# Strassen's scheme for the up projection of the last two token groups

## The chip, the cores and the metric

The kernel runs on one core of one Trainium2 chip. The metric is the device time of one execution in microseconds (us). All times below are of the whole program: one layer of a hybrid encoder on 2064 tokens (16 learned meta tokens and 2048 frames) of 1024 features.

## The reference

The layer has two halves. The first (two kinds of attention with one input and one output projection) is not touched by the change. The second is a gated network with a causal convolution of width 3 over the tokens:

```python
def _conv_ffn(x, w_in, conv_w, conv_b, w_out):
    h = x @ w_in                     # 1024 -> 5632: the up projection
    y = conv_b
    for i in range(CONV_W):          # three taps over tokens
        y = y + conv_w[i] * hp[:, i:i + L]   # hp: h after two zero tokens
    u, gt = jnp.split(y, 2, axis=-1)
    return (jax.nn.silu(gt) * u) @ w_out     # 2816 -> 1024: the down projection
```

It is applied to the normed stream after the attention's output projection `w_o` was added: `h = h + _conv_ffn(_rmsnorm(h, norm2_g[l]), ...)`. Everything is float32.

## The kernel before

TensorE multiplies in a reduced format (`float32r`), so each operand is split into two parts, `hi` (a cast on ScalarE) and `lo` (the rest, one subtraction on VectorE or GpSimd), and each product is made of three: hi·hi, hi·lo and lo·hi (`product`, L1091). A matmul has 128 rows of contraction, 128 output rows and up to 512 columns (tokens).

The tokens of the network's second half go in four groups (`FGROUPS`): 514, 512, 512 and 512 tokens. The first two run beside the second part of the attention; the last two run alone, from about 2,610 us to the end. A group does, in this order: the output projection `w_o` with the norm (8 blocks of 24 matmuls, then the normed activations as `xh` and `xl`), then 22 blocks f of the inner width in 11 pairs (`mlp`). `up(G, f)` makes two 128-row blocks of the up projection, u (block f) and g (block 22 + f): eight contraction tiles by three matmuls of 512 columns each, 48 in all for one f. Then come the convolution, the gate (tanh on ScalarE, two steps on VectorE) and the split of the result into `zh` and `zl`. `down(G, ...)` adds the pair's share to the 8 output blocks: 48 matmuls of 512 columns for a pair. The down of a pair is written behind the up of the next pair, and the last down of a group behind the `w_o` of the next group.

Weights come by SyncE's DMA queue as 128x1024 `ww_raw` tiles (512 KB; ring of 2) and are split whole into `ww_hi` and `ww_lo` (ring of 3). u and g need two of them for one f; the down needs two for a pair.

The state of the convolution between groups is in the tile `edge`: two columns for each block, already multiplied by the taps (four small GpSimd instructions for each block, L1179 to L1182).

The order of instructions on each engine is set by a list scheduler that plays the program, in its written order of priority, against a model of the engines; at run time each engine takes its instructions strictly in that order and waits at semaphores.

## Time and profile before

| | us |
|---|---|
| median of 3 runs | 3427.64 |
| lowest and highest run | 3419.93, 3429.69 |
| the profiled execution | 3421.68 |
| its span | 3419.8 |
| TensorE busy in the span | 3321.0 (97%) |
| VectorE, ScalarE, GpSimd busy | 2301.7, 1653.1, 1165.1 |
| granted TensorE clock, mean | 0.987 |

A span is the time from the first to the last instruction of the program. "PE" is TensorE, "PEld" its weight loads, "DVE" VectorE, "ACT" ScalarE, "POOL" GpSimd, "SP" SyncE. L1096 is a line of the kernel; every matmul of the second half has that one line, so they are told apart by their tiles: `pp<-xh,ww_hi` is an up projection of the last groups, `pr<-zh,ww_hi` a down projection. A matmul's recorded duration overlaps that of the next one; what a stream of them costs is read from start to start, or from the length of a run of them in the chain of waits.

### The profile page before, as it was taken

To read this page: it belongs to the slowest core of one execution; us is meant where nothing else is said; L and a number is where in the kernel's file an instruction comes from. 1 tells how busy PE (TensorE), PEld (TensorE's weight loads), DVE (VectorE), ACT (ScalarE), POOL (GpSimd) and SP (SyncE) were. 2 spreads that over 40 slices of the span, in tenths; PEclk is the share of its full clock that TensorE was granted. 3 is DMA by queue.
4 is the path that set the end of the run, shared out by engine and by line. 5 is a ranking of instruction groups with operands and counts; after the bars stand their busy time and mean duration, and the time that the engine had idled before them with its cause. 6 is when DMAs were issued, how large, how long until landed. Compare 5 with 4: busy or idle time off the path is not lost.

```text
span 3419.8 us, 62536 instructions
## 1 busy us (share of the span) xinstructions
PE 3321.0 (97%) x23259; PEld 2941.8 (86%) x23259; DVE 2301.7 (67%) x4849; ACT 1653.1 (48%) x3450; POOL 1165.1 (34%) x2055
## 2 busy tenths in 40 slices
PE   7999999999999999999999999999999999999999
PEld 7889888988988988999999998888887888878887
DVE  5655566566556657888878886777665666646666
ACT  5543444554244467765666665654333333333332
POOL 4441113344111167755444454422114211132121
PEclk9999999999999999999999999999999999999999
DMA  4556333355634255333333343223324323232222
GB/s 114 119 123 161 105 95 99 102 124 130 156 88 105 84 173 160 112 103 109 94 93 94 93 137 117 86 82 129 104 89 159 97 90 97 93 116 94 93 93 92
DMA packets 352888, 376.57 MB, mean 110 GB/s; under 512 B 169112, under 2 KB 281992, under 8 KB 351560
## 3 DMA queue, kind: packets, MB, share of 16 engines
q1 hardware_dynamic: 352392, 372.52, 38.2%
q8 instruction: 183, 3.00, 0.4%
q14 instruction: 121, 0.99, 0.1%
...
## 4 chain that ended last, share of the span: by engine, by line
PE 51%; DVE 2%; DMA 2%; POOL 2%; issue 2%; ACT 2%; SPq 0%; POOLq 0%; ACTq 0%; DVEq 0%
PE pp L1096 30%; PE pr L1096 12%; PE o L1022 3%; PE pt L1002 3%; DMA raw<-d_qk 2%; PE s L952 1%; PE s L954 1%; DVE ww_lo L82 1%; POOL xl L1158 0%; POOL kl L894 0%; DVE P L945 0%; DVE pl L1018 0%; ACT P L971 0%; DMA cb<-d_cd 0%; ACT ph L1017 0%
## 5 line engine op out<-in xcount | busy, mean ns | idle before, releaser
L82 DVE TENSOR_TENSOR ww_lo<-ww_raw,ww_hi 128x1024 fp32r<-128x1024 f32 (+1 forms) x304 | 375.4, 1244 | 248.7 <-PE pp L1096 128.9
L81 ACT CAST ww_hi<-ww_raw 128x1024 fp32r<-128x1024 f32 (+1 forms) x304 | 307.6, 1025 | 387.9 <-PE pp L1096 140.0
L1096 PE MATMUL pp<-xh,ww_hi 128*128 128x512 f32 (+2 forms) x1952 | 432.3, 353 | 11.4 <-ACT xh L1157 6.0
L1096 PE MATMUL pp<-xh,ww_lo 128*128 128x512 f32 (+2 forms) x1952 | 429.1, 351 | 0.0
L1096 PE MATMUL pp<-xl,ww_hi 128*128 128x512 f32 (+2 forms) x1952 | 428.4, 350 | 0.3 <-POOL xl L1158 0.3
L1096 PEld LDWEIGHTS pp<-xh,ww_hi 128*128 128x128 f32 x1952 | 324.8, 190 | 66.5 <-ACT xh L1157 11.1
L1096 PEld LDWEIGHTS pp<-xl,ww_hi 128*128 128x128 f32 x1952 | 326.2, 189 | 52.8 <-POOL xl L1158 1.0
L1096 PEld LDWEIGHTS pp<-xh,ww_lo 128*128 128x128 f32 x1952 | 325.3, 189 | 47.4
L1179 POOL TENSOR_SCALAR c<-c,pc 128x1 f32<-128x1 f32 x220 | 84.7, 385 | 611.2 <-ACT c L1176 609.8
L1018 DVE TENSOR_TENSOR pl<-pt,ph 128x512 fp32r<-128x512 f32 (+2 forms) x352 | 196.1, 562 | 51.7 <-ACT ph L1017 50.1
L1191 POOL TENSOR_TENSOR zl<-cv,zh 128x512 fp32r<-128x512 f32 (+1 forms) x110 | 119.8, 1089 | 312.7 <-ACT zh L1190 302.3
L945 DVE CUSTOM_DVE_ANT_0 P<-cb,s 16x16 f32<-16x16 f32 (+8 forms) x360 | 182.7, 519 | 53.6 <-PE s L954 29.1
L1017 ACT CAST ph<-pt 128x512 fp32r<-128x512 f32 (+2 forms) x352 | 167.8, 486 | 103.4 <-PE pt L1002 72.9
L1204 DVE TENSOR_TENSOR acc<-acc,pr 128x512 f32<-128x512 f32 x240 | 164.5, 688 | 73.5 <-PE pr L1096 69.1
L1002 PE MATMUL pt<-cst,P 128*128 128x128 f32 (+2 forms) x1224 | 202.6, 277 | 2.6 <-ACT P L971 1.5
L1173 ACT ACTIVATE cv<-pp,pc 128x510 f32<-128x510 f32 (+1 forms) x220 | 151.9, 691 | 84.3 <-PE pp L1096 82.9
L89 POOL TENSOR_TENSOR wi<-sq,kx 128x320 fp32r<-128x320 f32 (+2 forms) x48 | 48.2, 1003 | 389.9 <-ACT kx L88 290.1
L203 PE MATMUL pj<-xah,w_hi 128*128 128x384 f32 x480 | 165.8, 346 | 1.6 <-ACT xah L194 1.6
L1177 DVE SCALAR_TENSOR_TENSOR cv<-pp,pc,cv 128x511 f32<-128x511 f32 (+1 forms) x220 | 140.7, 639 | 36.0 <-ACT c L1176 35.9
L205 PE MATMUL pj<-xah,w_lo 128*128 128x384 f32 x480 | 164.4, 342 | 0.4 <-DVE w_lo L82 0.4
L204 PE MATMUL pj<-xal,w_hi 128*128 128x384 f32 x480 | 163.6, 341 | 0.0
L1022 PE MATMUL o<-ph,vs 128*128 128x256 f32 x576 | 158.1, 284 | 5.5 <-ACT ph L1017 5.2
...
## 6 DMA issues: line engine op xcount, KB each, us to landing
ww_raw<-in_fin_dram SPq DMA_DIRECT2D x176, 512.0 KB, 3.6
ww_raw<-in_fout_dram SPq DMA_DIRECT2D x88, 512.0 KB, 3.7
w_raw<-in_wt_dram SPq DMA_DIRECT2D x60, 512.0 KB, 3.8
...
ww_raw<-in_wo_dram SPq DMA_DIRECT2D x24, 512.0 KB, 3.6
...
```

The costliest lines, as they stand in the source:

```text
L81: nc.scalar.copy(hi, raw)
L82: nc.vector.tensor_sub(lo, raw, hi.bitcast(F32))
L203: nc.tensor.matmul(p, wh[:, c, :M], xh[:, c, :n], start=c == 0, stop=False)
L204: nc.tensor.matmul(p, wh[:, c, :M], xl[:, c, :n], start=False, stop=False)
L205: nc.tensor.matmul(p, wl[:, c, :M], xh[:, c, :n], start=False, stop=c == KC - 1)
L945: nc.vector.tensor_tensor_reduce(dst, c, src, 1.0, 3e38, op0=ALU.add, op1=ALU.min, accum_out=mx[:nq, np_ : np_ + 1])
L1002: nc.tensor.transpose(pt[:kn, x, c0 : c0 + nq], P[:nq, k0 : k0 + kn], K.ident[:nq, :nq])
L1017: nc.scalar.copy(ph[:kn, xs, c:N], pt[:kn, xs, c:N])
L1018: nc.vector.tensor_sub(pl[:kn, xs, c:N], pt[:kn, xs, c:N], ph[:kn, xs, c:N].bitcast(F32))
L1022: nc.tensor.matmul(o[:, c:N], vs[:kn, jj], pp[:kn, x, c:N], start=False, stop=jj == nt - 1 and y == 1)
L1096: self.K.nc.tensor.matmul(p, w, x, start=i == 0, stop=i == len(mms) - 1)
L1204: nc.vector.tensor_tensor(a, a, p, op=ALU.add)
```

## The change

For the last two groups (`win=True`) the up projection of one f is treated as a product of 2x2 blocks: the weights have rows u and g and two halves of the contraction (a11, a12 for u, a21, a22 for g), the activations two halves of the contraction and two halves of the tokens (b11 to b22). Strassen's scheme in Winograd's form gives the four result blocks from seven block products instead of eight, with sums of blocks before and after. A block product is 4 contraction tiles by three matmuls of 256 columns: 84 matmuls of 256 columns for one f, where there were 48 of 512.

- `operands`, once for a group: the four blocks of the normed activations are made in float32, four sums of blocks are formed on VectorE (t1 to t4), and the seven right-hand operands are split (`G.B`, seven hi and seven lo tiles of 128x1024; q0 to q6 are the hi parts, q7, q8, q12, q9, q14, q13, q10 the lo parts in the order of use).
- `up_win`, for each f: the two raw weight tiles `ru` (u) and `rg` (g) are loaded as before. Four sums of weight blocks are formed on GpSimd: s1 = a21 + a22 (L1252), then in place a21 = a11 - a21 (L1259), a11 = s1 - a11 (L1260), a12 = a12 - a11 (L1267). Seven 128x512 blocks w1 to w7 are split in four ring tiles (w1 and w5, w4 and w6, w2, w3 and w7); the lo parts of w6 and w3 are made on GpSimd, the others on VectorE. The seven products go to four PSUM banks of a ring of five. ScalarE (L1256, L1258, L1265, L1276) and VectorE (L1270, L1273, L1275, L1277) combine them into an SBUF tile `cc`, from which the convolution and the gate read.
- The edge is now the last two raw columns, copied in and out of `cc` by GpSimd (L1234, L1278); the second group writes it in that form (`carry`).
- `down` loads its weights in two halves of four output blocks, each from two DMAs of 256 KB, into a third raw buffer or the ring; the number of its matmuls is unchanged. The raw buffers are now three in turn; `ru` and `rg` are held until the sums and splits have read them.
- PSUM: `up` of these groups has the five banks and `down` the three, the other way round from before.

```diff
-        w = [self.weight(K.fout[f]) for f in fs]
+        w = [] if G.win else [self.weight(K.fout[f]) for f in fs]
...
+        nc.gpsimd.tensor_tensor(s1, a21, a22, op=ALU.add)
+        w1, w5 = pair((a11, nc.vector), (s1, nc.vector))
+        ba, bd = bank(), bank()
+        mm(ba, w1, B[0])
+        nc.scalar.copy(cu[:, lo], ba)
+        mm(bd, w5, B[1])
+        nc.scalar.copy(cg[:, hi], bd)
+        nc.gpsimd.tensor_sub(a21, a11, a21)
+        nc.gpsimd.tensor_sub(a11, s1, a11)
+        w4, w6 = pair((a22, nc.vector), (a11, nc.gpsimd))
+        bc = bank()
+        mm(bc, w4, B[2])
+        mm(ba, w6, B[3], False)
+        nc.scalar.copy(cu[:, hi], ba)
+        w2, = pair((a12, nc.vector))
+        nc.gpsimd.tensor_sub(a12, a12, a11)
+        bb = bank()
+        mm(bb, w2, B[4])
+        nc.vector.tensor_tensor(cu[:, lo], cu[:, lo], bb, op=ALU.add)
+        w3, w7 = pair((a12, nc.gpsimd), (a21, nc.vector))
+        mm(bd, w3, B[5], False)
+        nc.vector.tensor_tensor(cu[:, hi], cu[:, hi], bd, op=ALU.add)
+        mm(ba, w7, B[6], False)
+        nc.vector.tensor_tensor(cg[:, hi], cg[:, hi], ba, op=ALU.add)
+        nc.scalar.copy(cg[:, lo], ba)
+        nc.vector.tensor_tensor(cg[:, lo], cg[:, lo], bc, op=ALU.subtract)
+        nc.gpsimd.tensor_copy(edge, cc[:, :, 512:514])
...
+        for j, i in enumerate((f, FT + f)):
+            nc.scalar.activation(v[:, j], cc[:, j, 2:], AF.Identity, bias=pcol(K, "cb", i), scale=pcol(K, "cw2", i))
+            for k in (1, 0):
+                nc.vector.scalar_tensor_tensor(v[:, j], cc[:, j, k : k + 512], pcol(K, f"cw{k}", i), v[:, j], op0=ALU.mult, op1=ALU.add)
```

Two places show how the instructions stand. The first is GpSimd in the middle of the last group. Before, one f put this on it (`zl` of one f, then the four edge steps of a block of the next):

```order
L1191 TENSOR_TENSOR zl_6805_37482<-cv_6807_37508,zh_6804_37481 128x512
L1179 TENSOR_SCALAR c2_6837_37679<-c2_6837_37679,pc_11_70 128x1
L1180 TENSOR_SCALAR edge_2486_15450<-c2_6837_37679,pc_11_70 128x2
L1181 TENSOR_TENSOR edge_2486_15450<-edge_2486_15450,c2_6837_37679 128x1
L1182 TENSOR_TENSOR edge_2486_15450<-edge_2486_15450,pc_11_70 128x1
```

Now, from the last split of a pair's first f (the lo part of w3, `ww_lo_7140`) over its second f (raw tiles `ww_raw_7144` for u and `ww_raw_7145` for g; `sqv` is s1):

```order
L1245 TENSOR_TENSOR ww_lo_7140_40309<-ww_raw_7125_40213,ww_hi_7139_40308 128x512
L1252 TENSOR_TENSOR sqv_7146_40361<-ww_raw_7145_40358 128x512
L1278 COPY edge_2486_15450<-cc_7128_40218 128x2x2
L1259 TENSOR_TENSOR ww_raw_7145_40358<-ww_raw_7144_40357,ww_raw_7145_40358 128x512
L1260 TENSOR_TENSOR ww_raw_7144_40357<-sqv_7146_40361,ww_raw_7144_40357 128x512
L1267 TENSOR_TENSOR ww_raw_7144_40357<-ww_raw_7144_40357 128x512
L1245 TENSOR_TENSOR ww_lo_7153_40402<-ww_raw_7144_40357,ww_hi_7152_40401 128x512
L1234 COPY cc_7180_40584<-edge_2486_15450 128x2x2
L1245 TENSOR_TENSOR ww_lo_7159_40453<-ww_raw_7144_40357,ww_hi_7158_40452 128x512
L1290 TENSOR_TENSOR zl_7143_40354<-vv_7141_40343,zh_7142_40353 128x512
```

One 512-wide step for an f has become seven, and the copy of the first f's edge (L1278) stands between s1 and the other sums of the second f; it waits for VectorE's L1275 of the first f, the step that reads that f's last product. `ww_raw_7145` lies in the buffer that `ww_raw_7125` held, so its DMA waits for the first row.

The second place is TensorE at the same point. Before, one block of u and the block of g beside it:

```order
L1096 MATMUL pp_6835_37651<-xh_6512_35767,ww_hi_6828_37639 128x512 x8
L1096 MATMUL pp_6835_37651<-xl_6513_35768,ww_hi_6828_37639 128x512 x8
L1096 MATMUL pp_6835_37651<-xh_6512_35767,ww_lo_6829_37640 128x512 x8
L1096 MATMUL pp_6838_37687<-xh_6512_35767,ww_hi_6831_37645 128x512 x8
L1096 MATMUL pp_6838_37687<-xl_6513_35768,ww_hi_6831_37645 128x512 x8
L1096 MATMUL pp_6838_37687<-xh_6512_35767,ww_lo_6832_37646 128x512 x8
```

Now, from the lo part of the first f's w3 into the second f (`ww_hi_7148` holds w1 and w5 of the second f, `ww_hi_7152` w4 and w6, `ww_hi_7155` w2):

```order
L1109 MATMUL pr_7132_40228<-q5_6653_36903,ww_lo_7140_40309 128x256 x4
L1109 MATMUL pr_7131_40227<-q10_6656_36908,ww_hi_7139_40308 128x256 x2
L1109 MATMUL pr_7131_40227<-q6_6655_36907,ww_lo_7140_40309 128x256 x4
L1109 MATMUL pr_7150_40371<-q0_6640_36869,ww_lo_7149_40366 128x256 x4
L1109 MATMUL pr_7151_40372<-q1_6643_36883,ww_hi_7148_40365 128x256 x4
L1109 MATMUL pr_7151_40372<-q8_6644_36884,ww_hi_7148_40365 128x256 x4
L1109 MATMUL pr_7154_40407<-q2_6646_36889,ww_hi_7152_40401 128x256 x4
L1109 MATMUL pr_7154_40407<-q12_6647_36890,ww_hi_7152_40401 128x256 x4
L1109 MATMUL pr_7154_40407<-q2_6646_36889,ww_lo_7153_40402 128x256 x4
L1109 MATMUL pr_7157_40438<-q4_6651_36899,ww_hi_7155_40433 128x256 x4
L1109 MATMUL pr_7157_40438<-q14_6652_36900,ww_hi_7155_40433 128x256 x3
L1109 MATMUL pr_7151_40372<-q1_6643_36883,ww_lo_7149_40366 128x256 x4
```

The third row is the end of the first f's products. Behind the last row come the hi part of w6, its lo part (`ww_lo_7153`, made on GpSimd), the rest of w2 and w3; only then the first matmuls of a down projection. In the first f of a pair, 30 to 36 of the pair's 48 down matmuls stand between the up products.

## Rows read from the trace of the kernel before

**Rows 1.** The page: busy time of each engine; lines of the chain of waits.

```profile
PE 3321.0 (97%) x23259; PEld 2941.8 (86%) x23259; DVE 2301.7 (67%) x4849; ACT 1653.1 (48%) x3450; POOL 1165.1 (34%) x2055
...
PE pp L1096 30%; PE pr L1096 12%; PE o L1022 3%; PE pt L1002 3%; DMA raw<-d_qk 2%; PE s L952 1%; PE s L954 1%; DVE ww_lo L82 1%; POOL xl L1158 0%; POOL kl L894 0%; DVE P L945 0%; DVE pl L1018 0%; ACT P L971 0%; DMA cb<-d_cd 0%; ACT ph L1017 0%
```

**Rows 2.** Chain that ended last: start us, length us, of one pair; the end.

```profile
2704.01 11.15 PE pr L1096 x48
2715.16 22.50 PE pp L1096 x96
...
3393.06 22.30 PE pr L1096 x96
```

**Rows 3.** Busy time of each engine in that pair's 33.65 us.

```profile
core 0: us, PE busy (x) PEld busy (x) DVE busy (x) ACT busy (x) POOL busy (x), PEclk, DMA share, GB/s
2704.01:2737.66 33.65, 33.65 (x145) 27.14 (x145) 21.66 (x30) 12.13 (x18) 6.34 (x18) 1.00 0.29 95
```

**Rows 4.** Timeline of PE in group one, 256 columns: start, length (us), row, count.

```profile
1492.54 1.12 PE L1096 MATMUL pp<-xl,ww_hi 128*128 128x256 f32 x8
1493.49 0.28 PE L1096 MATMUL pp<-xh,ww_lo 128*128 128x256 f32 x1
```

**Rows 5.** Groups on DVE from 2340 us, by shape: count | busy us, mean ns.

```profile
L82 DVE TENSOR_TENSOR ww_lo<-ww_raw,ww_hi 128x1024 fp32r<-128x1024 f32 x187 | 232.7, 1257 | 220.1 <-PE pp L1096 124.0 <-ACT ww_hi L81 91.9 <-PE pr L1096 2.8
L1204 DVE TENSOR_TENSOR acc<-acc,pr 128x512 f32<-128x512 f32 x240 | 164.5, 688 | 73.5 <-PE pr L1096 69.1
...
L1188 DVE SCALAR_TENSOR_TENSOR cv<-cv,cv 128x512 f32<-128x512 f32 x58 | 40.7, 702 | 24.8 <-ACT cv L1187 24.0
```

**Rows 6.** The same on DVE from 1340 to 1420 us: 256 wide.

```profile
L1156 DVE SCALAR_TENSOR_TENSOR cv<-acc,pc,pp 128x256 f32<-128x256 f32 x8 | 3.4, 470 | 0.0
...
L1129 DVE TENSOR_TENSOR acc<-acc,pp 128x256 f32<-128x256 f32 x8 | 3.3, 413 | 0.5 <-PE pp L1096 0.5
```

**Rows 7.** The same on POOL from 2340 us.

```profile
L1191 POOL TENSOR_TENSOR zl<-cv,zh 128x512 fp32r<-128x512 f32 x58 | 75.5, 1301 | 247.0 <-ACT zh L1190 238.5 <-ACT c L1176 8.4
...
L1180 POOL TENSOR_SCALAR edge<-c,pc 128x2 f32<-128x2 f32 x114 | 33.3, 292 | 0.0
...
L1117 POOL TENSOR_TENSOR yl<-acc,yh 128x1024 fp32r<-128x1024 f32 x8 | 22.5, 2837 | 1.2 <-ACT yh L1116 1.1
```

**Rows 8.** The same on ACT from 1340 to 2340 us.

```profile
L1017 ACT CAST ph<-pt 128x256 fp32r<-128x256 f32 x47 | 17.5, 371 | 19.8 <-PE pt L1002 19.6
...
L1190 ACT CAST zh<-cv 128x512 fp32r<-128x512 f32 x8 | 5.0, 623 | 1.8 <-DVE cv L1189 1.7
```

**Rows 9.** Timeline of DVE at 2355 us and 3060 us: start, length (us).

```profile
2355.16 2.33 DVE L1189 SCALAR_TENSOR_TENSOR cv<-cv,cv 128x512 f32<-128x512 f32 x1
...
3059.56 0.75 DVE L1177 SCALAR_TENSOR_TENSOR cv<-pp,pc,cv 128x511 f32<-128x511 f32 x1 [0.39 <-ACT c L1176]
3060.22 1.21 DVE L82 TENSOR_TENSOR ww_lo<-ww_raw,ww_hi 128x1024 fp32r<-128x1024 f32 x1
```

**Rows 10.** Timeline of POOL at the same two places.

```profile
2348.29 8.66 POOL L1117 TENSOR_TENSOR yl<-acc,yh 128x1024 fp32r<-128x1024 f32 x3
2356.95 0.77 POOL L1179 TENSOR_SCALAR c<-c,pc 128x1 f32<-128x1 f32 x1
...
3059.63 0.34 POOL L1179 TENSOR_SCALAR c<-c,pc 128x1 f32<-128x1 f32 x1 [4.35 <-ACT c L1176]
3059.94 0.30 POOL L1180 TENSOR_SCALAR edge<-c,pc 128x2 f32<-128x2 f32 x1
3060.32 1.17 POOL L1181 TENSOR_TENSOR edge<-edge,c 128x1 f32<-128x1 f32 x1
3061.45 0.19 POOL L1182 TENSOR_TENSOR edge<-edge,pc 128x1 f32<-128x1 f32 x1
```

**Rows 11.** DMA issues of the page: count, size, us from issue to landing.

```profile
ww_raw<-in_fin_dram SPq DMA_DIRECT2D x176, 512.0 KB, 3.6
```

**Rows 12.** Busy times around the starts of the third and fourth group (columns as rows 3).

```profile
2612.56:2640.57 28.01, 23.77 (x94) 17.53 (x93) 18.32 (x20) 14.72 (x20) 23.64 (x14) 0.94 0.58 205
3036.09:3062.24 26.15, 23.90 (x101) 17.09 (x100) 14.22 (x21) 10.56 (x15) 15.87 (x14) 1.00 0.32 110
```

More of the change, by code (lines that the diff above doesn't have):

```diff
@@ L1158, in w_o, with operands, parts, scaled @@
                 nc.gpsimd.tensor_sub(G.xl[:, c, bs], x, G.xh[:, c, bs].bitcast(F32))
+    def operands(self, G, rs):
+        K, nc = self.K, self.K.nc
+        slot = lambda i, dt=F32: G.x([128, 2, 514], f"q{i}", dt=dt).rearrange("p a t -> p (a t)")[:, :1024].rearrange(
+            "p (c t) -> p c t", t=256)
+        b11, b12, b21, b22 = (slot(i) for i in (8, 9, 10, 11))
+        free = iter(range(7))
+        def parts(v, to, eng):
+            h, l = slot(next(free), F32R), slot(to, F32R)
+            nc.scalar.copy(h, v)
+            eng.tensor_sub(l, v, h.bitcast(F32))
+            return h, l
+        def scaled(c):
+            for j, b in enumerate(((b11, b12), (b21, b22))[c // 4]):
+                ts = slice(256 * j, 256 * j + 256)
+                nc.vector.scalar_tensor_tensor(b[:, c % 4], G.acc[:, c, ts], pcol(K, "g2", c), rs[:, ts], op0=ALU.mult, op1=ALU.mult)
+        def minus(a, b, i):
+            t = slot(i)
+            nc.vector.tensor_sub(t, a, b)
+            return t
+        for c in range(4):
+            scaled(c)
+        t1 = minus(b12, b11, 12)
+        p1 = parts(b11, 7, nc.gpsimd)
+        for c in range(4, KC):
+            scaled(c)
+        t2 = minus(b22, t1, 13)
+        p5 = parts(t1, 8, nc.vector)
+        t4 = minus(t2, b21, 14)
+        p4 = parts(t4, 12, nc.vector)
+        t3 = minus(b22, b12, 15)
+        p6 = parts(t2, 9, nc.gpsimd)
+        p2 = parts(b21, 14, nc.vector)
+        p3 = parts(b22, 13, nc.gpsimd)
+        p7 = parts(t3, 10, nc.vector)
+        G.B = [p1, p5, p4, p6, p2, p3, p7]
```

95 lines of the change are left out of this document (80 added, 15 removed).

## The prediction

> **What bounds the kernel now.** I read the page's shares first: TensorE is busy for 97% of the span, and the up projection alone (`pp L1096`) carries 30% of the chain of waits [rows 1]. An average can hide a stage with another limit, so I read the chain in the last two groups, the only place that the change reaches. There it is TensorE without a break: 11.15 us of down and 22.50 us of up for each pair of f [rows 2], and the busy times of such a pair show 33.65 us of TensorE in 33.65 us at a granted clock of 1.00, beside 21.66 us of VectorE, 12.13 us of ScalarE and 6.34 us of GpSimd [rows 3]. So every column that TensorE is spared there is worth its full time, until another engine or a wait needs more than what is left. That second question decides this case.
>
> **What TensorE saves.** A 512-column matmul costs 22.50 / 96 = 0.234 us. For 256 columns the trace has eight in a row that start 0.95 us before the next row, 0.119 us each [rows 4]: half, with no fixed part to speak of. A pair of f has 2 x 84 = 168 of them: 168 x 0.119 = 20.0 us against 22.50, a gain of 2.5 us a pair. With the down unchanged, a pair needs 31.1 us of TensorE where it took 33.65. Over 2 groups of 11 pairs that is 55 us, the ceiling of the gain.
>
> There is a statement against this. The Trainium skill's page "TensorE: Matmul & The Clock Gate" (section "Back-to-back issue gap") gives 81 ns for 128 and 131 ns for 512 columns in streams of weight loads and matmuls; a line through these would put 256 columns at some 98 ns, an estimate, and 168 small ones would then cost 3.9 us more a pair than 96 large ones. The trace has 234 ns and 119 ns for the two sizes, so I give that rule no weight.
>
> **What the other engines get, for one f.** VectorE: five lo parts, four convolution steps and two gate steps, 11 x 0.70; one 1024-wide lo part of the down, 1.26; four sums out of PSUM, 4 x 0.41; four additions to `acc`, 4 x 0.69 [rows 5, 6]. That is 13.4 us, 26.7 a pair where it was 21.66. ScalarE: seven casts and four other 512-wide steps at 0.62, four PSUM copies at 0.37 [rows 8] and a 1024-wide cast (about 1.05, from twice the 0.62 less one start): 9.4 us, 18.8 a pair. GpSimd: four sums, two lo parts and `zl`, 7 x 1.30, and two edge copies at about 0.29 [rows 7]: 9.7 us, 19.4 a pair where it was 6.34. Each alone fits into 31.1 us. Three things make it tight.
>
> **First, VectorE and GpSimd exclude each other on SBUF.** The gate step at 2355.16 took 2.33 us instead of 0.70: a GpSimd step held until 2356.95, and the gate step ended 0.54 us behind that. At 3060.32 a GpSimd step on one column took 1.17 us instead of 0.19, until the lo part on VectorE was done. The step that reads PSUM (L1177, 0.75 us) ran beside GpSimd undisturbed [rows 9, 10]. In the new up, nearly all that VectorE does has both inputs in SBUF; the convolution, which read PSUM before, now reads `cc`. Added up with full durations, the two need 11 x 0.70 + 1.26 on VectorE and 9.7 on GpSimd, 18.7 us for one f, 37.3 a pair, one after the other. When they queue, the start of a step is hidden (0.54 instead of 0.70; I take 0.15 off each): 15.7 us, 31.5 a pair. So this alone needs between 31.5 and 37.3 us a pair. The Trainium skill says the same in "SBUF — State Buffer" (section "Who interferes with whom"): a VectorE instruction with two SBUF inputs and a GpSimd instruction that reads SBUF block each other, whichever starts second; were the rows an accident, GpSimd's work would lie beside VectorE's and a pair would stay at TensorE's 31.1 us, which is my first rival.
>
> **Second, the raw weights go round a loop.** The second f's `rg` lies in the buffer of the first f's `ru`, which is free only when GpSimd has made the lo part of w3. From there: DMA 3.6 [rows 11], s1, three sums, two lo parts (6 x 1.30) and two copies (0.6), 12.0 us, to the same step of the second f. From that to the first f of the next pair: two loads in a row (3.6 and some 2 more, an estimate), the six steps and `zl` of the f before (7 x 1.30) and the copies: 15.3. The loop needs 27.3 us a pair without any waiting, and 34.5 if each of its 13 steps finds one 0.55 us step of VectorE ahead of it.
>
> **Third, the second f of a pair has nothing to fill with.** Call T the end of the first f's products. In TensorE's order 43 matmuls, 5.1 us, follow before the lo part of w6 is needed, and no down matmul is among them. On GpSimd, between T and that lo part: VectorE's L1275 (0.41), the edge copy (0.29), three sums and the lo part (4 x 1.30): 5.9 us undisturbed, 8.1 with one VectorE step ahead of each. And the w5 product needs s1: 3.6 + 1.30 + 0.62 = 5.5 us behind the lo part of w3, where TensorE has only 14 matmuls, 1.7 us, if it waits for that lo part itself; if it comes later, the gap shrinks one for one. These gaps overlap, they don't add. I put the second f at 3.4 us (bounds 0.6 and 6), the first f, with 7 to 8 us of down matmuls in between, at 1 (0 and 2). So a pair takes 31.1 + 4.4 = 35.5 us (31.7 to 39). That is inside the band of the first limit (31.5 to 37.3) and a little over the second's upper end, which is where loops that depend on each other end up. For 20 pairs with a down: 20 x 4.4 = 88 us of waiting.
>
> **Group starts.** Before, TensorE was idle for 4.24 and 2.25 us there (28.01 - 23.77, 26.15 - 23.90) [rows 12]. Now 16 scaled blocks (0.47 each [rows 6]), four sums and four lo parts of 1024 (1.26 each) are on VectorE, 17.6 us, and three lo parts of 1024 on GpSimd (2.84 each [rows 7]), 8.5, which exclude each other for the most part. The first f (10 us of products) needs the last of them, so it ends some 20 to 26 us behind the norm: 10 to 16 us of waiting, 13 as the middle. The second f has no down to lean on either: 5 more (2 to 8). Less the idle before, 3.2 on average: +15 for each group (9 to 21), 30 in all. The end keeps its cover: the last two downs, 22.30 us in a row [rows 2], lose at most 2 to 3 us to the longer way from the last product to `zl`; I count none.
>
> **The sum.** 3421.7 (the profiled execution) - 55 + 88 + 30 = 3485. The median of the runs lies 6 us above that execution, so I say 3487: 1.7% slower. Everything ahead of 2,100 us stands in the same order as before and costs nothing.
>
> **The rivals.**
> - *TensorE stays the bound* (faster). The loop and the port just fit, a pair takes 31.1 to 32.5 us, the starts cost 8 us each: 3421.7 - 55 + (0 to 28) + 16 = 3383 to 3411, say 3397. For it: each engine's own sum fits, the raw loop without waiting is 27.3, and the first f's down matmuls are a good cover. Against it: the rows on exclusion, and a second f with no cover. It wins if a pair stays under 32.5 us. Chance 0.20.
> - *The waits just eat the gain*: about 33 us a pair, 3412 to 3438, no change by 0.3% (about what a measurement can tell here). Chance 0.08.
> - *The middle case*, a pair at 34 to 37 us: 3450 to 3515, 3487 as its middle. Chance 0.55, the small gap between 33 and 34 included.
> - *VectorE and GpSimd become the bound* (slower still). If their steps follow each other with full durations, 37.3 us a pair, and VectorE stands at PSUM reads that TensorE delivers late: 37.3 to 39 us, 20 x 3.7 to 5.4 and 30 to 40 for the starts, 3525 to 3570. It decides where the two have no free moment left. Chance 0.17.
> - *That the change doesn't do what it says*: the matmuls are there as written (84 of 256 columns for one f), so I give this nothing.
>
> **How the numbers follow.** Likeliest: the middle case, 3487. Faster by over 0.3%: 0.20, same 0.08, slower 0.72. For 8 in 10 the range has to reach into the fast rival and over part of the slow one: 3395 to 3540; the middle case's own range is 3450 to 3515.
>
> **What would show it.** Right: in the middle of the last group the chain of waits of the changed kernel is no longer one row of TensorE but breaks at each second f, with GpSimd's L1245, L1259, L1260 or the DMA of `in_fin` in it; a pair lasts over 34 us; lo parts and gate steps on VectorE average clearly over 0.70 us, GpSimd's sums over 1.30; the product stream stays at 0.119 us a matmul. Wrong in the gain's term: more than 0.125 us for one of 256 columns. Wrong in the waits: TensorE busy throughout a pair, VectorE's steps near 0.70. Wrong in the starts: less than 6 us of idle TensorE at the two group starts.

## The result

The changed kernel takes **3584.2 us** (median; 3582.5 to 3591.8) where the kernel before takes 3428.7 in the same comparison: a ratio of **1.0472**, 95% interval 1.0447 to 1.0497. Slower was forecast, but at 3487, which is 58 us more than before, and at 3540 at most; it is 156 more.

The page of the changed kernel answers to [rows 1]: shares of busy time, the chain that ended last by line, and the costliest group (busy us, mean ns, then the idle time just before it and what ended it).

```profile
PE 3334.5 (93%) x24843; PEld 3032.3 (85%) x24843; DVE 2571.2 (72%) x5101; ACT 1784.4 (50%) x3756; POOL 1495.5 (42%) x1913
...
PE pp L1109 20%; PE pr L1109 5%; DVE vv L1283 3%; DVE ww_lo L1245 3%; PE o L1022 3%; PE pt L1002 2%; DVE acc L1353 2%; DMA ww_raw<-in_fin_dram 2%; DMA raw<-d_qk 2%; PE s L952 1%; PE s L954 1%; DMA ww_raw<-in_fout_dram 1%; POOL ww_lo L1245 1%; ACT ww_hi L1244 1%; POOL zl L1290 1%
...
L1109 PE MATMUL pr<-q,ww_hi 128*128 128x256 f32 x2464 | 391.1, 308 | 127.5 <-ACT ww_hi L1244 110.3
```

TensorE's share falls from 97% to 93%, and the chain now passes through VectorE, GpSimd and transfers. One line names the place: the hi products wait 127.5 us, 110.3 of them for ScalarE's cast of a weight block.

The next view gives busy times by stretch, as [rows 3]. The first two stretches are nine pairs of f in the third and in the fourth group, from f = 2 to f = 20 (from one copy of the first product, L1256, to another). Then come one wait inside a pair and what follows it, and the two group starts.

```profile
core 0: us, PE busy (x) PEld busy (x) DVE busy (x) ACT busy (x) POOL busy (x), PEclk, DMA share, GB/s
2664.00:3024.50 360.50, 307.04 (x1939) 281.44 (x1938) 291.39 (x357) 162.70 (x293) 213.60 (x165) 0.91 0.24 80
3163.60:3517.20 353.60, 300.34 (x1916) 274.19 (x1917) 295.43 (x357) 161.91 (x291) 218.72 (x165) 0.94 0.25 81
3254.00:3260.50 6.50, 2.63 (x23) 2.43 (x21) 4.14 (x7) 2.55 (x5) 2.43 (x3) 1.00 0.47 164
3260.58:3264.00 3.42, 3.42 (x16) 3.42 (x17) 3.42 (x3) 0.62 (x3) 3.34 (x4) 0.51 0.00 0
...
2600.00:2664.00 64.00, 40.45 (x226) 36.52 (x225) 51.22 (x56) 24.15 (x36) 44.94 (x27) 0.76 0.41 135
...
3092.00:3163.60 71.60, 59.95 (x327) 51.88 (x325) 51.17 (x64) 26.99 (x42) 37.80 (x26) 0.90 0.26 89
```

A pair takes 360.5 / 9 = 40.1 us in the third group and 39.3 in the fourth, where it took 33.65 [rows 3]. TensorE is idle for (360.50 - 307.04) / 9 = 5.9 us of it, 5.9 in the fourth group as well, and its busy time is 34.1 and 33.4 us, not the 31.1 that the work needs: the granted clock is 0.91 and 0.94. The two short rows show one such place. TensorE works for 2.63 of 6.5 us, still at a granted clock of 1.00, and in the 3.42 us that follow the clock is 0.51, the 1.2 GHz level. Here the wait is paid a second time; e4 below puts that to a test.

The same columns from 2600 us to the end, for the changed kernel and then for the kernel before:

```profile
2600.00:3580.80 980.80, 822.65 (x5020) 741.66 (x5018) 783.46 (x955) 424.87 (x738) 562.73 (x418) 0.92 0.26 85
```

```profile
2600.00:3419.80 819.80, 808.86 (x3451) 649.03 (x3449) 511.86 (x704) 293.99 (x434) 196.23 (x429) 1.00 0.32 102
```

With these rows the loss adds up. TensorE is idle for 158.2 us where it was 10.9, so 147 more: 20 x 5.9 = 118 us in the twenty pairs with a down, and 29 us at the group starts (23.6 and 11.7 us instead of 4.24 and 2.25 [rows 12]). It is also busy for 14 us more, though 55 us of work were saved, so for 69 us that the work does not need. Of these, 10 x 3.0 + 10 x 2.3 = 53 us lie in the pairs and 16 outside of them. An estimate from the granted clock gives about as much: (1 - 0.91) x 34.1 = 3.1 and (1 - 0.94) x 33.4 = 2.0 us a pair, and (1 - 0.76) x 40.45 + (1 - 0.90) x 59.95 = 16 us at the starts. Idle and busy time together make 161 us, which is what the two profiled executions differ by.

**What ends the wait.** Waits of the changed kernel in these two groups (us in total, times, longest):

```profile
PE pr L1109 <- ACT ww_hi L1244: 95.3, 39, 5.6
...
POOL sqv L1252 <- DMA ww_raw<-in_fin_dram: 80.9, 19, 5.7
POOL cc L1234 <- DVE vv L1286: 80.7, 25, 11.2
POOL ww_raw L1267 <- DVE ww_lo L1245: 57.2, 18, 3.8
```

Nineteen times, once a pair, GpSimd stands 4.3 us before s1 until a raw block has landed. The timeline of such a place (start us, length; in brackets the idle time before and its releaser; VectorE first, then GpSimd, SyncE's queue, ScalarE, TensorE):

```profile
3281.85 1.19 DVE L1283 SCALAR_TENSOR_TENSOR vv<-cc,pc,vv 128x512 f32<-128x512 f32 x1
3282.96 0.68 DVE L1245 TENSOR_TENSOR ww_lo<-raw,ww_hi 128x512 fp32r<-128x512 f32 x1
3283.56 0.74 DVE L1283 SCALAR_TENSOR_TENSOR vv<-cc,pc,vv 128x512 f32<-128x512 f32 x1
3284.22 1.27 DVE L1353 TENSOR_TENSOR acc<-acc,pp 128x512 f32<-128x512 f32 x2
3285.42 0.68 DVE L1245 TENSOR_TENSOR ww_lo<-ww_raw,ww_hi 128x512 fp32r<-128x512 f32 x1
...
3286.18 1.67 POOL L1267 TENSOR_TENSOR ww_raw<-ww_raw 128x512 f32<-128x512 f32 x1 [3.69 <-DVE ww_lo L1245]
...
3289.13 1.28 POOL L1290 TENSOR_TENSOR zl<-vv,zh 128x512 fp32r<-128x512 f32 x1 [0.69 <-ACT zh L1289]
3290.37 1.73 POOL L1245 TENSOR_TENSOR ww_lo<-ww_raw,ww_hi 128x512 fp32r<-128x512 f32 x1
3296.14 1.26 POOL L1252 TENSOR_TENSOR sqv<-ww_raw 128x512 f32<-128x512 f32 x1 [4.04 <-DMA ww_raw<-in_fin_dram]
...
3292.13 0.33 SPq L1228 DMA_DIRECT2D ww_raw<-in_fin_dram  x1
...
3280.14 1.23 ACT L1244 CAST ww_hi<-ww_raw 128x512 fp32r<-128x512 f32 x2 [0.96 <-POOL ww_raw L1260]
...
3297.72 0.63 ACT L1244 CAST ww_hi<-sqv 128x512 fp32r<-128x512 f32 x1
...
3298.40 1.86 PE L1109 MATMUL pr<-q,ww_hi 128*128 128x256 f32 x7 [4.15 <-ACT ww_hi L1244]
```

Read it upward from the last row: TensorE waits for the cast of s1, this for s1, s1 for the DMA, the DMA for the lo part of the first f's w3 at 3290.37 (it held the buffer), this for a12' at 3286.18 and for `zl` ahead of it, and a12', which is written over a12, for VectorE's lo part of w2 at 3285.42. The cast that this lo part needs had ended at 3281.37 (3280.14 + 1.23); it then stood in VectorE's queue behind taps, another lo part and additions to `acc`. Two theories follow. **The raw-buffer loop** (theory 1): the order in which raw buffers come free sets the pair. **The lock** (theory 2): VectorE and GpSimd shut each other out of SBUF, and the stretched steps set it. The groups of both engines over these stretches (xcount | busy us, mean ns):

```profile
L1283 DVE SCALAR_TENSOR_TENSOR vv<-cc,pc,vv 128x512 f32<-128x512 f32 x162 | 185.5, 1146 | 16.4 <-ACT vv L1281 15.9
L1245 DVE TENSOR_TENSOR ww_lo<-ww_raw,ww_hi 128x512 fp32r<-128x512 f32 x120 | 134.1, 1118 | 33.2 <-ACT ww_hi L1244 33.0
...
L1287 DVE SCALAR_TENSOR_TENSOR vv<-vv 128x512 f32<-128x512 f32 x40 | 35.0, 874 | 0.8
L1286 DVE SCALAR_TENSOR_TENSOR vv<-cc,vv 128x512 f32<-128x512 f32 x40 | 28.4, 710 | 9.4 <-ACT cc L1285 9.4
...
L1273 DVE TENSOR_TENSOR cc<-cc,pr 128x256 f32<-128x256 f32 x41 | 17.0, 416 | 4.5 <-PE pr L1109 4.2
...
L1245 POOL TENSOR_TENSOR ww_lo<-ww_raw,ww_hi 128x512 fp32r<-128x512 f32 x78 | 118.7, 1527 | 20.9 <-ACT ww_hi L1244 16.1 <-PE pr L1109 1.9 <-PE pp L1109 1.9
```

VectorE's taps and the largest group of its lo parts take 1.15 and 1.12 us where 0.70 was counted [rows 5], GpSimd's lo parts 1.53 instead of 1.30 [rows 7]; the step that reads PSUM still takes 0.42. The two gate steps also have both inputs in SBUF, but L1287 takes 0.87 us and L1286 only 0.71. GpSimd's next step, L1234, waits for L1286 (80.7 us in all), so GpSimd often stands still while that step runs; this fits theory 2.

### The profile page after: what moved, and what is told of

It reads as the page before. It is cut to its first block, busy times and chain, and to the rows that moved or that the text cites. A ratio compares the mean times of both kernels' runs of the same rounds, so it can differ in the third digit from the quotient of the medians.

```text
span 3580.8 us, 66516 instructions
## 1 busy us (share of the span) xinstructions
PE 3334.5 (93%) x24843; PEld 3032.3 (85%) x24843; DVE 2571.2 (72%) x5101; ACT 1784.4 (50%) x3756; POOL 1495.5 (42%) x1913
## 3 DMA queue, kind: packets, MB, share of 16 engines
q1 hardware_dynamic: 358728, 372.52, 35.9%
## 4 chain that ended last, share of the span: by engine, by line
PE 33%; DVE 11%; POOL 5%; issue 5%; DMA 5%; ACT 3%; SPq 0%; POOLq 0%; ACTq 0%; DVEq 0%
PE pp L1109 20%; PE pr L1109 5%; DVE vv L1283 3%; DVE ww_lo L1245 3%; PE o L1022 3%; PE pt L1002 2%; DVE acc L1353 2%; DMA ww_raw<-in_fin_dram 2%; DMA raw<-d_qk 2%; PE s L952 1%; PE s L954 1%; DMA ww_raw<-in_fout_dram 1%; POOL ww_lo L1245 1%; ACT ww_hi L1244 1%; POOL zl L1290 1%
## 5 line engine op out<-in xcount | busy, mean ns | idle before, releaser
L1109 PE MATMUL pr<-q,ww_hi 128*128 128x256 f32 x2464 | 391.1, 308 | 127.5 <-ACT ww_hi L1244 110.3
L1109 PEld LDWEIGHTS pr<-q,ww_hi 128*128 128x128 f32 x2464 | 359.2, 213 | 148.3 <-ACT ww_hi L1244 122.8
L1109 PE MATMUL pp<-xh,ww_hi 128*128 128x256 f32 (+2 forms) x1248 | 248.6, 326 | 4.7 <-ACT xh L1177 1.7
L1109 PE MATMUL pp<-xh,ww_lo 128*128 128x256 f32 (+2 forms) x1248 | 250.3, 325 | 0.0
L1109 PE MATMUL pp<-xl,ww_hi 128*128 128x256 f32 (+2 forms) x1248 | 248.3, 325 | 0.0
L1353 DVE TENSOR_TENSOR acc<-acc,pp 128x512 f32<-128x512 f32 (+1 forms) x376 | 203.1, 553 | 24.8 <-PE pp L1109 24.0
L1283 DVE SCALAR_TENSOR_TENSOR vv<-cc,pc,vv 128x512 f32<-128x512 f32 x176 | 204.6, 1164 | 18.6 <-ACT vv L1281 18.0
L1109 PE MATMUL pr<-q,ww_lo 128*128 128x256 f32 x1232 | 201.3, 291 | 15.0 <-POOL ww_lo L1245 8.4
L1109 PE MATMUL pp<-zh,ww_hi 128*128 128x512 f32 (+2 forms) x752 | 206.5, 355 | 6.0 <-DVE acc L1353 3.0
L1109 PE MATMUL pp<-zl,ww_hi 128*128 128x512 f32 (+1 forms) x752 | 198.9, 345 | 0.0
```

Source lines behind the costliest of these rows:

```text
L1109: self.K.nc.tensor.matmul(p, w, x, start=start and i == 0, stop=i == len(mms) - 1, skip_group_check=not start)
L1283: nc.vector.scalar_tensor_tensor(v[:, j], cc[:, j, k : k + 512], pcol(K, f"cw{k}", i), v[:, j], op0=ALU.mult, op1=ALU.add)
L1353: nc.vector.tensor_tensor(a, a, p, op=ALU.add)
```

## The experiments

A pair is measured as above, from f = 2 to f = 20. "Idle" is the part of a pair in which TensorE does not work, from the same stretches. Part of one pair's down lies outside of each stretch: the stretches of e14, say, hold 1916 and 1909 matmuls, where nine pairs have 9 x (168 + 48) = 1944. So every pair in the table is low, by an estimated 0.4 to 0.9 us, and differences of under half a microsecond between two rows mean nothing. Most kernels were timed once, beside the kernel before on the same chip; the time of one kernel moves by up to 0.8% from execution to execution (the kernel before took 3405.2 to 3432.3 us beside e12). Four kernels, e11 to e14, were timed several times and have a ratio with its 95% interval.

| kernel | total us | before | pair, third / fourth group | idle a pair | clock |
|---|---|---|---|---|---|
| changed kernel | 3584.2 | 3428.7 | 40.1 / 39.3 | 5.9 / 5.9 | .91 / .94 |
| e1 deep raw buffers, fourth group | 3545.5 | 3428.3 | 40.3 / 34.8 | 6.5 / 2.7 | .93 / .98 |
| e2 a12' into s1's buffer | 3503.6 | 3428.3 | 36.2 / 35.8 | 3.9 / 3.7 | .98 / .99 |
| e3 without two taps | 3508.8 | 3428.3 | 36.8 / 35.6 | 3.9 / 3.1 | .97 / .98 |
| e4 wait filled with products | 3606.0 | 3428.3 | 41.3 / 40.5 | 4.4 / 3.7 | .98 / .99 |
| e5 = e1 + e2 | 3509.5 | 3410.4 | 36.1 / 35.4 | 3.9 / 2.9 | .98 / .98 |
| e6 = e2 + e3 | 3434.9 | 3410.4 | 32.9 / 32.0 | 1.4 / 1.0 | .98 / 1.00 |
| e7 = e2, fills for three sums | 3409.9 | 3410.4 | 31.5 / 30.9 | 0.5 / 0.4 | .99 / .99 |
| e8 = e7, longer fills | 3421.8 | 3425.6 | 31.5 / 32.0 | 0.6 / 0.8 | .99 / .99 |
| e10 fills, old buffer | 3497.7 | 3425.6 | 35.0 / 35.9 | 3.1 / 3.6 | .97 / .95 |
| e9 sums made once | 3534.5 | 3425.6 | 30.6 / 30.4 | 0 / 0 | .99 / 1.00 |
| e11 the same, own buffers | 3426.4 | 3418.2 | 30.7 / 30.3 | 0.1 / 0 | .99 / 1.00 |
| e12 the same, from blocks at hand | 3457.4 | 3418.6 | 30.7 / 30.5 | 0.1 / 0 | .99 / 1.00 |
| e13 first six f's later | 3450.5 | 3420.8 | 30.7 / 30.3 | 0.1 / 0 | .99 / 1.00 |
| e14 sums spread evenly | 3403.5 | 3417.5 | 30.5 / 30.3 | 0 / 0 | .99 / 1.00 |

### Is it the loop? e1, e2, e5

e1, in the last group alone:

```diff
+    def deep():
+        k, calls[0] = calls[0], calls[0] + 1
+        if k < 2:
+            return W([128, 1024], "ww_raw", F.rings[1])
+        return L([128, 2, 514], f"q{(k - 2) % 8}").rearrange("p a t -> p (a t)")[:, :1024]
...
-        G.z, G.raw = L, raw
+        G.z, G.raw = L, (deep if i else raw)
```

> Everything is computed; only the buffers change: in the last token group alone the raw weights, after its first two blocks, take turns in eight dead y tiles instead of the three raw buffers, so that no load waits for a split. Theory 1 (the loop through three raw buffers sets the wait before the second f of a pair): the last group's pair, 39.3 us in the changed kernel, falls to 36 or less, and the whole time by 25 to 45 us from 3584 (about 3545). Theory 2 (VectorE and GpSimd shut each other out of SBUF and their work sets the pair): the pair stays at 38 to 39.5 us and the time within 10 us of 3584, since no work is taken away. Group 3, which is untouched, stays at 40 us a pair under both.

e2, in both groups:

```diff
-        nc.gpsimd.tensor_sub(a12, a12, a11)
+        nc.gpsimd.tensor_sub(s1, a12, a11)
...
-        w3, w7 = pair((a12, nc.gpsimd), (a21, nc.vector))
+        w3, w7 = pair((s1, nc.gpsimd), (a21, nc.vector))
```

> Everything is computed; the difference a12' = a12 - a11' is written into the buffer of s1, which is free by then, and no longer over a12. So GpSimd's subtraction no longer waits for VectorE's lo of w2 to have read a12, and the raw buffer comes free without the split of w3. Theory 1 (raw-buffer loop): the wait before the second f falls by the time from a12's last reading to the end of the lo of w3, 3 to 5 us a pair in both groups; pair 35 to 37 us, total about 3500 to 3530. Theory 2 (exclusion): no work goes, pair stays at 38.5 to 40, total within 15 us of 3584.

Busy times over the nine pairs of each group, e1 first, then e2 (columns as before):

```profile
2671.30:3033.50 362.20, 303.63 (x1938) 277.04 (x1938) 293.03 (x357) 162.80 (x292) 214.50 (x165) 0.93 0.24 80
3176.10:3488.90 312.80, 288.06 (x1920) 262.10 (x1921) 290.73 (x359) 158.70 (x292) 218.70 (x164) 0.98 0.28 92
```

```profile
2654.80:2980.40 325.60, 290.35 (x1925) 263.62 (x1926) 300.10 (x359) 160.12 (x290) 214.23 (x166) 0.98 0.28 88
3121.00:3442.80 321.80, 288.32 (x1924) 260.44 (x1923) 291.37 (x356) 157.24 (x290) 214.43 (x165) 0.99 0.28 89
```

Both land where theory 1 said. e1 changes the fourth group alone, from 39.3 to 34.8 us, and the untouched third stays at 40.3: this is the same work with more buffers. e2 changes which buffer one result goes into and takes 81 us off the kernel. The clock rises with the waits gone, to 0.98. But the pair does not come down to TensorE's 31: VectorE is now busy for 300.1 of 325.6 us.

e5 puts both edits together, to see whether the loop holds anything back once e2 is in.

> Everything is computed; both earlier edits together: a12' goes into the buffer of s1, and in the last group the raw weights take turns in eight dead y tiles. If the raw-buffer loop still holds part of the 35.8 us that the last group's pair takes with the first edit alone: pair 32 to 34.5 us, total 3465 to 3490. If the loop is broken already and VectorE with GpSimd's locks (its rows stand at 91% of those pairs) is next: pair 35 to 36 us, total within 12 us of 3504.

The fourth group's pair goes from 35.8 to 35.4 us only: the loop is broken by e2 already, and something else holds the pair at 36.

### Is it the lock? e3, e6, e7, e8, e10

e3 leaves two convolution taps of each block out, e6 does so on top of e2:

```diff
-            for k in (1, 0):
-                nc.vector.scalar_tensor_tensor(v[:, j], cc[:, j, k : k + 512], pcol(K, f"cw{k}", i), v[:, j], op0=ALU.mult, op1=ALU.add)
```

> Left out: the two earlier taps of the convolution, four VectorE steps of 512 columns an f (1.1 us each in the changed kernel's trace, 9 us a pair). Theory 2 (VectorE and GpSimd together set the pair): GpSimd and VectorE are each other's hindrance, so the pair falls from 39.5 by 5 us or more, total under 3490. Theory 1 (raw-buffer loop): only the part of VectorE's queue that stands ahead of the lo of w2 shortens the loop; pair falls by 1 to 3 us, total 3520 to 3560. If neither decided: no change.

> a12' goes into the buffer of s1, and left out are the two earlier taps of the convolution (four VectorE steps an f). If VectorE with GpSimd's locks is what is late once the raw-buffer loop is broken: pairs fall from 36.2 and 35.8 us to 31 to 33.5, near TensorE's 31.1, total 3420 to 3460. If something else (loads, ScalarE's order) holds the pair at 36: pairs stay above 35, total above 3485.

Pairs of 36.8 and 35.6 us in e3, 3.3 and 3.7 less than in the changed kernel: between what the two theories said, which does not decide, as VectorE's queue is part of the loop too. Total 3509, nearer theory 1. With the loop broken (e6) the same edit brings the pair to 32.9 and 32.0: VectorE's load was what was late there. Whether it is its own work or the lock, e7 tells: it takes no work from VectorE at all. GpSimd's three sums that follow s1 are replaced:

```diff
-        nc.gpsimd.tensor_sub(a21, a11, a21)
-        nc.gpsimd.tensor_sub(a11, s1, a11)
+        for t in (a21, a11):
+            for _ in range(2):
+                nc.gpsimd.memset(t, 0.5)
...
-        nc.gpsimd.tensor_sub(a12, a12, a11)
+        for _ in range(2):
+            nc.gpsimd.memset(s1, 0.5)
```

> a12' goes into the buffer of s1, and left out are three of GpSimd's four block sums an f: in their place GpSimd fills the same blocks with a constant, twice over, so that it stays busy for about as long (two fills of 64x512 took 2 x 0.53 us in the kernel's trace, a sum 1.3 to 1.7) and still writes before the casts, but reads nothing from SBUF. If GpSimd's reading shuts VectorE out (theory 2): VectorE's split step in the pairs falls towards its 0.68 us from about 1.1 in the changed kernel, and the pair falls by 1.5 to 4 us, total 3420 to 3475. If GpSimd's length alone counts: VectorE's steps keep their mean, pair within 0.7 us of 36, total within 15 us of 3504.

> As the run with two fills in place of each of three block sums (pair 31.5 and 30.9 us against 36.2 and 35.8 with the sums), but with three fills, 3 x 0.526 = 1.58 us, as long as the sums took there (1.50 to 1.75 us); left out are these three sums. If it was GpSimd's reading of SBUF that held the pair (theory 2): pair stays at 31 to 32 us, VectorE's taps stay near 1.06 us, total within 15 us of the two-fill run. If it was the length of GpSimd's steps (1.05 us for two fills against 1.5): pair goes back to 34 to 36 us, total 3460 to 3500.

e7 and then e8 (three fills for each sum) over the nine pairs:

```profile
2660.60:2944.00 283.40, 278.50 (x1924) 258.79 (x1925) 253.56 (x360) 157.97 (x292) 172.46 (x222) 0.99 0.32 101
3076.10:3353.90 277.80, 274.14 (x1908) 255.16 (x1908) 249.21 (x356) 157.34 (x289) 169.00 (x217) 0.99 0.32 103
```

```profile
2664.00:2947.80 283.80, 278.09 (x1927) 259.09 (x1927) 253.53 (x358) 161.84 (x292) 198.83 (x273) 0.99 0.32 101
3078.60:3366.20 287.60, 280.74 (x1929) 258.76 (x1928) 264.25 (x362) 161.09 (x293) 196.76 (x276) 0.99 0.31 100
```

The groups of e8 from 2680 to 2960 us, the taps of VectorE and one of GpSimd's fills:

```profile
L1285 DVE SCALAR_TENSOR_TENSOR vv<-cc,pc,vv 128x512 f32<-128x512 f32 x72 | 59.5, 849 | 12.6 <-ACT vv L1283 11.9
...
L1269 POOL MEMSET sqv<- 128x512 f32 x54 | 28.4, 527 | 1.0 <-DVE ww_lo L1245 0.2
```

In e7 the pair is 31.5 and 30.9 us, with TensorE idle for 0.5 and 0.4 us of it: close to TensorE's bound, and a larger fall (4.7 and 4.9 us from e2) than I had expected. VectorE's busy time for the same 360 steps falls from 300.1 us (e2) to 253.6. In e8 GpSimd is kept as long as by the sums (3 x 0.527 us against 1.5 to 1.75), and the pair stays within 1.1 us of e7's: so it is not the length of GpSimd's steps but that they read SBUF. The Trainium skill, "SBUF — State Buffer" (section "Who interferes with whom"), says that a VectorE instruction with two SBUF inputs contends with a GpSimd instruction that reads SBUF and not with one that only writes it. The traces agree: VectorE is busy for 253.5 and 264.3 us in e8, for 300.1 and 291.4 in e2, which has the same buffers. The mean of one group of steps says less. From 2680 to 2960 us the taps take 1.39 us in e2, 1.06 in e7 and 0.85 in e8, where I had expected no change between the last two. GpSimd still has four steps for each f that read SBUF (s1, two lo parts, `zl`), and which of VectorE's steps run beside these shifts from kernel to kernel.

e10 completes the square: fills, but with a12' over a12, as in the changed kernel.

> The changed kernel's own buffers (a12' over a12), but three of the four block sums an f are left out: two fills of the same block stand in each one's place. This keeps the raw-buffer loop and takes the reading away. If loop and lock add up: the pair keeps the loop's 3.9 us over the 31.2 of the run without both, so about 35 us, total 3480 to 3500. If the loop is only as long as the lock makes it (its steps wait in VectorE's queue): pair 31 to 33 us, total 3410 to 3445.

35.0 and 35.9 us, 3.5 and 5.0 more than e7: the loop costs its share without these three sums' reading too. TensorE's wait only moves, to ScalarE's copy of the first product (L1256: 52.3 us in 20 waits from 2664 to 3440 us); in the place at 2820 us that copy stood behind casts of the raw block that the loop brings late. Third group: 40.1 us with both, 36.2 without the loop, 35.0 without the reading, 31.5 without either; the two causes add up there (3.9 + 5.1 = 9.0 against 8.6). Fourth group: 39.3, 35.8, 35.9 and 30.9. There each remedy alone gives less (3.5 + 3.4 = 6.9 against 8.4), so that part of the loss goes only with both. In neither group is one cause hidden behind the other.

### Is the wait paid twice? e4

Three more products of w1 in every second f, into the bank that the s1 product then overwrites:

```diff
+        if f % 2:
+            for _ in range(3):
+                mm(bd, w1, B[0])
         mm(bd, w5, B[1])
```

> Work is added: in every second f of a pair the product w1 B11 is repeated three more times (36 matmuls of 256 columns, 36 x 0.119 = 4.3 us a pair) into the bank that the s1 product then overwrites; the output stays the reference's. It fills the wait of about 4 us that stands there. Theory 3 (each wait is paid twice, the second time as a stretch at half clock behind it, about 2.5 us a pair): the added matmuls run inside the wait, the half-clock stretch behind it goes, and the time falls by 20 to 50 us although 94 us of matmuls are added. If the half clock comes from something else than the wait: the time stays or rises, by up to 94 us if the wait does not shrink in turn.

```profile
2660.50:3032.60 372.10, 332.83 (x2272) 303.31 (x2271) 300.27 (x360) 164.81 (x296) 210.67 (x166) 0.98 0.24 78
3180.30:3544.60 364.30, 330.84 (x2260) 301.48 (x2261) 305.42 (x360) 160.34 (x291) 213.24 (x166) 0.99 0.24 79
```

These are e4's pairs. The gain that I expected did not come: the kernel is 22 us slower. Half of the theory holds: the clock goes from 0.91 and 0.94 to 0.98 and 0.99, and 94 us of added matmuls cost 22. In a pair, 4.3 us of matmuls were added; TensorE's busy time grew by only 2.9 and 3.4 us and its idle time fell by 1.6 and 2.2, to 4.4 and 3.7, so the pair grew by 1.2 to 1.3. The pair did not get shorter, which fits a period that is set by the other engines' loop. e4 does not show that by itself, since the added products also stand ahead of the s1 product in TensorE's order.

### Is the scheme itself slower? e9, e11 to e14

The block sums of the weights are the same for both groups, and for every f they are made twice. e9 makes them once, in place in the raw buffers of the second group's up stage, stores them to DRAM, and the last two groups load them:

```diff
+        if G.carry:
+            (a11, a12), (a21, a22) = ((r[:, 0:512], r[:, 512:1024]) for _, _, r in w)
+            nc.gpsimd.tensor_tensor(a22, a21, a22, op=ALU.add)
+            nc.gpsimd.tensor_sub(a21, a11, a21)
+            nc.gpsimd.tensor_sub(a11, a22, a11)
+            nc.gpsimd.tensor_sub(a12, a12, a11)
+            for j, (_, _, r) in enumerate(w):
+                nc.sync.dma_start(K.ws[f, :, 1024 * j : 1024 * j + 1024], r)
```

> Everything is computed, but the four block sums of the weights are made once, in the up stage of the second token group (where GpSimd is busy 18 to 29% and TensorE 100% of the time), stored to DRAM, and loaded by the last two groups in place of the raw block a21: seven blocks an f come in instead of eight quarter sums being made there. If theory 2 holds and the second group's VectorE has room (54 to 69% busy): pair 30.9 to 32.5 us as in the run with fills, the second group not longer by more than 10 us, total 3390 to 3440 and so within 0.5% of the kernel before on either side. If the added loads (0.8 MB an f) or the single SyncE queue become the bound: pair 34 us or more, total above 3470.

e9's busy times in the second group's up stage and in the nine pairs of the third group, then the changed kernel's in that second group:

```profile
2400.00:2600.00 200.00, 153.25 (x557) 117.99 (x556) 84.89 (x117) 47.98 (x70) 52.13 (x53) 0.84 0.32 105
2798.10:3073.40 275.30, 275.30 (x1916) 257.15 (x1916) 249.36 (x361) 160.43 (x291) 101.59 (x92) 0.99 0.51 159
```

```profile
2400.00:2600.00 200.00, 200.00 (x858) 161.17 (x857) 117.66 (x160) 69.49 (x101) 25.07 (x35) 1.00 0.29 95
```

The pairs run at TensorE's bound, 275.30 of 275.30 us. The price is in the second group, where TensorE falls from 100% to 77%, and the third group's nine pairs begin at 2798 us instead of 2664, where I had allowed 10 us at most. The second group's own weights wait for raw buffers that the sums and stores hold, as the longest wait of SyncE's queue from 2400 to 2600 us says (L78 loads the weights; us in total, times, longest):

```profile
SPq L78 <- DMA d_ws<-ww_raw: 57.2, 16, 5.0
```

e11 gives the sums loads and buffers of their own (eight q tiles), e12 takes the blocks at hand and writes into the q tiles, e13 makes the first six f's sums a little later, e14 the first eleven, one f at a time:

```diff
+        if G.carry and f >= 11:
+            self.sums(f, [t[2] for t in w], [G.s(10 + (2 * f + j) % 6) for j in range(2)])
+        if G.carry and 10 <= f < 21:
+            rs = [G.s(8 + j) for j in range(2)]
+            for r, i in zip(rs, (f - 10, FT + f - 10)):
+                nc.sync.dma_start(r, K.fin[i].rearrange("p c f -> p (c f)"))
+            self.sums(f - 10, rs, rs)
```

> Everything is computed. As the run that makes the four block sums once, in the second token group's up stage (its last two groups ran at 30.5 us a pair, but the second group's up stage became 140 us longer, since the sums kept the two raw buffers that its own weights need). Here the sums have buffers of their own, eight q tiles that the last two groups need only later, and their own loads of the weight blocks. If the raw buffers were the cause: the second group's up stage is back within 10 us of the kernel before, pairs stay at 30.4 to 30.7 us, total 3385 to 3415, faster than the kernel before by 0.4 to 1.2%. If GpSimd's reading there, or the added loads and stores (2 MB an f), hold the second group up: total 3440 to 3530.

> Everything is computed. The four block sums are again made once in the second group's up stage, but from the weight blocks that are there anyway (no loads of their own) and into eight q tiles that the last groups need only later, so that the two raw buffers are held for GpSimd's four sums (about 6 us) and not for the store as well. In the run with loads of its own the sums ran as one burst at 2310 to 2500 us (GpSimd 91%, DMA 98% busy) and TensorE's share fell to 87% there. If that burst was the cost: the second group's up stage loses under 15 us against the kernel before, pairs stay at 30.3 to 30.7 us, total 3385 to 3410, ratio 0.990 to 0.997. If GpSimd's reading slows VectorE's weight splits in that stage whenever it happens, or the raw buffers are still held too long: ratio 1.000 to 1.025.

> Everything is computed. As the run before (sums made once in the second group's up stage, from the weight blocks that are there: pairs 30.6 us, TensorE 100% busy at 2300 to 2600 us, but 74% at 2200 to 2300, where GpSimd's first sum waited 21 us for memory that the attention before still held), with the first six f's sums made a little later from loads of their own, so that nothing of the second group waits for that memory. If that wait was the cost: TensorE's share at 2200 to 2300 us is back at 95% or more, total 3400 to 3425, ratio 0.994 to 1.001. If the scheme loses as much elsewhere as the pairs gain (group starts, the burst of six f's own loads): ratio 1.002 to 1.010.

> Everything is computed. As the run before, but the second group's first eleven f's are left as they were, and their sums are made from loads of their own one f at a time, beside the later eleven f's (whose sums come from the blocks that are there); so neither a wait for memory (10 us before the first sum, then 18 us of TensorE) nor a burst of loads (75% DMA at 2300 to 2400 us) stands in the second group. If these two were what that stage lost: TensorE's share at 2200 to 2600 us is 97% or more everywhere, pairs stay at 30.3 to 30.8, total 3395 to 3415, ratio 0.992 to 0.998, and what is left of the scheme's loss are its group starts (idle and half clock about 30 us more than before). If making the sums costs the second group as much wherever they stand (two f's sums an f, some 11 us of GpSimd in 21, and 250 GB/s): ratio 1.002 to 1.012.

- e11: ratio 1.0026 (1.0012 to 1.0039). The sums run as one burst.
- e12: 1.0116 (1.0093 to 1.0140). TensorE 100% busy from 2300 to 2600 us, but a wait ahead of that.
- e13: 1.0087 (1.0065 to 1.0108). The wait has only moved.
- e14: **0.9962** (0.9948 to 0.9977): 0.4% faster than the kernel before, a small step but clear of its interval, and 5% faster than the changed kernel by the two ratios (0.9962 / 1.0472).

e11 came out between the two times that I had named for it, e12 and e13 at the slower of their two, e14 at the faster.

The stretch that lost in each, e11, e12, e13; then e14's second group from 2300 to 2600 us and its two group starts:

```profile
2300.00:2500.00 200.00, 179.45 (x781) 143.09 (x779) 131.42 (x164) 65.83 (x103) 148.48 (x114) 0.95 0.81 307
```

```profile
2200.00:2300.00 100.00, 73.65 (x362) 58.38 (x362) 53.83 (x112) 43.80 (x73) 43.38 (x38) 0.90 0.39 134
```

```profile
2300.00:2400.00 100.00, 62.58 (x247) 48.29 (x246) 40.61 (x50) 25.74 (x37) 76.15 (x55) 0.81 0.75 276
```

```profile
2300.00:2600.00 300.00, 289.07 (x1257) 232.83 (x1256) 201.30 (x255) 106.01 (x162) 181.36 (x141) 0.98 0.61 216
...
2620.00:2679.20 59.20, 44.59 (x272) 39.53 (x271) 49.94 (x60) 26.03 (x41) 32.10 (x20) 0.92 0.57 184
3020.00:3084.90 64.90, 55.47 (x323) 49.30 (x322) 47.52 (x65) 26.89 (x44) 25.54 (x18) 0.89 0.39 126
```

In all four the pair is 30.3 to 30.7 us by the table; they differ in what the second group pays. Six whole pairs, from f = 8 to f = 20 in e14's fourth group, take 185.80 / 6 = 31.0 us each:

```profile
3171.70:3357.50 185.80, 185.80 (x1300) 173.26 (x1300) 170.71 (x242) 105.42 (x194) 65.19 (x60) 1.00 0.48 155
```

e14 still pays 11 us of idle TensorE in the second group, and its group starts are idle for 14.6 and 9.4 us, 18 more than [rows 12]. What the clock takes there (0.92, 0.89 and 0.98) is some 15 us, an estimate made as above. Of the 55 us that the pairs save, 11 should then be left; the medians differ by 14. So the scheme as such is not slower here: what made the changed kernel slow is that its sums are made beside the pairs. (e9 to e14 no longer write a12' over a12 either, so both causes go at once in them.)

## Why the prediction was right and wrong

- **Direction and mechanism**: right. All three "things that make it tight" are in the trace, and most of what was named as proof is there: the chain breaks at each second f, with L1245 and the DMA of `in_fin` in the broken place, and VectorE's taps and lo parts average 1.1 us. For the gate steps the sign came only in part (0.87 and 0.71 us).
- **Where the 98 us went**: the sum gave 3485 for an execution like the profiled one, and the changed kernel's took 3582.6. Of the difference, 30 us are waits in the pairs (118 instead of 88) and 69 are busy time of TensorE beyond what its work needs; the group starts give back 1. (With the 6 us that the text names, 3485 would have become 3491 and not 3487; that changes nothing.)
- **What TensorE saves**: right to 0.1 us. A whole undisturbed pair takes 31.0 us (e14), and 31.1 was said.
- **First reason, the lock**: right and sized well: 31.5 to 37.3 us a pair was said, and with the loop broken (e2) a pair takes 36.2 and 35.8. e8 adds what no row of before could show, that a GpSimd step which only writes does not hold VectorE.
- **Second reason, the loop, and the step from it to the pair**: this step failed. I priced the loop at 27.3 us without waiting and 34.5 with one VectorE step of 0.55 us ahead of each of its steps, and took a pair of 35.5 us, inside the lock's band and a little over the loop's upper end, as the place "where loops that depend on each other end up". With three of the four sums' reading taken away, the loop gives 35.0 and 35.9 us (e10), near my upper price. With the reading it gives 40.1 and 39.3: the two causes add, in the third group in full (e2, e7, e10), where I let the one stand inside the other. The queue shows how: a12' waited 3.7 us for the lo part of w2, which stood behind several steps of VectorE, taps and additions to `acc` among them, and not behind one; and `zl`, which waits for the gate, stands on GpSimd ahead of the lo part of w3.
- **Third reason, no cover in the second f**: the right place; 5.9 us idle a pair instead of 4.4. The long wait is the one for s1, ahead of the w5 product (3.94 and 4.15 us in two places), not the one for the lo part of w6, which I had put first.
- **The clock**: this step failed too, and it is the larger error. It was put at nothing: [rows 3] showed 1.00, and I left it there though I forecast waits of 3 to 4 us, and though [rows 12] had a granted clock of 0.94 in the stretch with 4.24 us of idle TensorE. The runs showed 0.91 and 0.94 in the pairs and 0.76 and 0.90 at the starts, which is most of the 69 us.
- **Group starts**: 30 us of waiting were forecast, 29 came, but unevenly (19 and 9), so that the sum is that close by some luck; the slow clock there was again not in it.
- **The rivals**: "VectorE and GpSimd become the bound" gave 3525 to 3570 with 0.17, and came nearest, with the wrong inside: its pair of 37.3 to 39 us came from full durations one after the other, while in the trace a loop of buffers and the lock add up to 40. The range, 3395 to 3540, ended too low, for want of the clock and of a sum of the two causes.
